# A transformer layer in float32 on one core: when DMA-made weight sums of the first Strassen group are loaded

## Chip, core and metric

The kernel runs on one core of a Trainium2 chip. The metric is the device time of one execution in microseconds (us). Before the change it is 1293.23 us, the median of three runs (1292.48 to 1294.61). Engines are named as the profile names them: PE (TensorE, matmuls), DVE (VectorE), ACT (ScalarE), POOL (GpSimd), SP (SyncE, which here only issues DMAs). A DMA that adds to its destination is issued by POOL.

## What is computed

One layer on x of 512 tokens by 1024 features, all in float32:

```python
x = x + 0.5 * swiglu(rmsnorm(x, ffn1_norm), ffn1_w1, ffn1_w3, ffn1_w2)   # first feed-forward
h = rmsnorm(x, mix_norm)
x = x + hybrid_mixer(h, w_in, ...)          # dilated attention, grouped-query attention, gates
x = x + 0.5 * swiglu(rmsnorm(x, ffn2_norm), ffn2_w1, ffn2_w3, ffn2_w2)   # second feed-forward
return rmsnorm(x, final_norm)

def swiglu(x, w1, w3, w2):                  # w1, w3: 1024 x 2816, w2: 2816 x 1024
    return (silu(x @ w1) * (x @ w3)) @ w2
```

## The kernel before

**Products.** Each product of float32 numbers is made of three matmuls of a shorter format: an operand is split into a high part H (a copy on ACT, `wh` for weights, L211) and a low part L (a subtraction on DVE, `wl`, L212), and `mm3` (L226 to L228) adds H·H, L·H and H·L in a PSUM bank. A weight tile is thus loaded (512 KB), cast on ACT, split on DVE, and then used by 24 matmuls on PE. The split tiles have a ring of three buffers (`wh`), so a tile's cast waits until PE has finished with the tile three before it; in feed-forward stages every fourth tile of the order uses a buffer of its own (`whx`).

**A feed-forward stage** (`ffn_run`) has a plain part and groups. In the plain part of the first feed-forward (stage "a") eight weight tiles, the first four feature blocks of w1 and w3, are multiplied with the 512 tokens, 24 matmuls of 128x512 each; the first two go pairwise. The four banks of `mm` rotate. A finished bank is emptied on DVE by `done1` (L445: times R, the norm's factor per token) or `done3` (L449), with a silu on ACT between. R comes late: the squares are summed, POOL takes the power (L380, `r`), PE transposes it (L395, `rb`), ACT copies it to R (L397). Until then the four banks are full.

**The groups** make blocks of w1 and w3 by a Strassen scheme, two at a time (f and f+1) in seven steps of 24 matmuls of 128x256: A11, S1, S2, A12, S3, S4, A22. GROUPS gives the groups' ends: in stage "a" the first group has f = 4 and 6, in stage "b" (the second feed-forward) f = 2, 4 and 6; the second starts at f = 8 in both. The weights of the steps are:

- A11 and A12: a plain load by SP (L190) into one of three `wa` tiles; A22 into a `wr` tile;
- S1 and S3: sums of two quarters, made by DMA in one of four `wt` tiles. SP loads the first quarter (L192); when that has landed POOL issues an accumulating DMA of the second (L193);
- S2 = S1 + A11 and S4 = S2 + A12: sums on DVE (L210, `ws`).

**The order of the loads.** `Layer.order` lists all weight tiles as PE uses them, numbered n. In stage "a" n = 0 to 7 are the plain tiles; the first group has n = 8 (A11 of f=4), 9 (S1), 10 (S2), 11 (A12), 12 (A11 of f=6), 13 (S3 of f=4), 14 (S1 of f=6), up to 21. `todo` (L117) is the sequence in which the loads are written into the program: by n, but a `wt` tile is sorted as if it were EARLY steps sooner. `loads` takes from its head as long as the ring has a tile. PE's order is the program's own; on the other engines a scheduler sets the order when the program is built, from the sequence in which it was written and its own estimate of when inputs are there. Each engine and each queue then runs strictly in that order.

```python
EARLY = {"a": 6, "b": 6, "q": 4}
GROUPS = {"a": (4, 8, 16, 22), "b": (2, 8, 16, 22)}
...
self.todo = sorted((n for n, t in enumerate(self.kind) if t != "ws"),
                   key=lambda n: n - (EARLY[self.order[n][0][2]] if self.kind[n] == "wt" else 0))
```

Of the kernel before, what the change touches and what calls it, by code (L numbers as in the profile page):

```python
# [16 lines left out]
DRAM = bass.MemoryType.DRAM  # L17

BUFS = {"wr": 3, "wa": 3, "ws": 2, "wt": 4, "wh": 3, "whx": 1}
EARLY = {"a": 6, "b": 6, "q": 4}  # L20
GROUPS = {"a": (4, 8, 16, 22), "b": (2, 8, 16, 22)}
PAIRS = ((0, 0), (1, 0), (0, 1), (0, 2), (1, 1), (1, 2), (2, 0), (3, 0), (2, 1), (2, 2), (3, 1), (3, 2))
NSQ = 10
# [46 lines left out]
class Layer:  # L70
    def __init__(self, ctx, tc, a):
        self.tc, self.nc, self.a = tc, tc.nc, a
        ctx.enter_context(tc.manual_schedule(engines={mybir.EngineType.PE}))
        pool = lambda n, **k: ctx.enter_context(tc.tile_pool(name=n, **k))
        self.dram = pool("dram", bufs=1, space=DRAM)
        self.cst = pool("cst", bufs=1)
        self.wb = pool("wb", bufs=1)
        self.tmp = pool("tmp", bufs=4)
        self.psm = pool("psm", bufs=4, space=PSUM)
        self.psa = pool("psa", bufs=4, space=PSUM)  # L80
        nc = self.nc
        c = self.cst
        self.x = [c.tile([128, T], F32, name=f"x{d}") for d in range(NK)]
        self.par = c.tile([128, 48], F32, name="par")
        nc.scalar.dma_start(self.par, a["par"])
        self.ident = c.tile([128, 128], F32, name="ident")
        self.ones = c.tile([128, 1], F32, name="ones")
        nc.vector.memset(self.ones, 1.0)
        self.mhalf = c.tile([128, 4], F32, name="mhalf")
        nc.vector.memset(self.mhalf, -0.5)  # L90
        nc.scalar.activation(self.ones, self.ones, AF.Copy)
        self.r = c.tile([128, 8], F32, name="r")
        self.R = c.tile([128, T], F32, name="R")
        nc.gpsimd.memset(self.R, 0.0)
        self.acc = c.tile([128, T], F32, name="acc")
        self.open_h()
        self.gate_d = self.dram.tile([16, 128, T], F32, name="gate_d")
        self.qk_d = self.dram.tile([2 * NSQ, 128, T], F32, name="qk_d")
        self.items = ([("v", 0), ("v", 1), ("sw", 0), ("v", 2)] + [("g", j) for j in range(2)]
                      + [("qk", f) for f in range(NSQ, 12)] + [("g", j) for j in range(2, 9)]  # L100
                      + [("b", g) for g in range(3)] + [("g", j) for j in range(9, 16)])
        span = {"v": ("wav", 4), "qk": ("waq", 2), "g": ("wg", 1), "b": ("wb", 4)}
        self.order = self.ffn_order("a")
        for kind, n in self.items:
            if kind == "sw":
                self.order += [("swq", at) for at in self.slots(range(0, NSQ, 2))]
                continue
            name, m = span[kind]
            self.order += [(name, m * n + i) for i in range(m)]
        self.order += [("wab", i) for i in range(12)] + [("wo", i) for i in range(8)]  # L110
        self.order += self.ffn_order("b")
        self.raws, self.tiles, self.used, self.wx, self.TQ = {}, [], 0, None, None
        self.cap = len(self.order)
        self.rings = {k: [] for k in BUFS}
        self.index = {it[:2]: n for n, it in enumerate(self.order)}
        self.kind = [self.home(it) for it in self.order]
        self.todo = sorted((n for n, t in enumerate(self.kind) if t != "ws"), key=lambda n: n - (EARLY[self.order[n][0][2]] if self.kind[n] == "wt" else 0))  # L117

    @staticmethod
    def slots(fs):  # L120
# [1098 lines left out]
```

## Time and profile before

| | |
|---|---|
| median of three runs | 1293.23 us |
| the profiled execution | 1292.9 us |
| its span | 1291.1 us |
| PE busy | 1270.1 us (98%) |
| DVE, ACT, POOL busy | 889.5, 587.0, 118.5 us |
| mean granted clock of PE | 0.993 of full speed |
| moved by DMA | 181.91 MB, mean 141 GB/s |

The profile is of one execution. A row gives a start and a duration in us from the span's start; in brackets stands how long the engine was idle before, and what ended that. PE's rows overlap, since matmuls are pipelined: from start to start counts. The granted clock is the share of TensorE's full 2.4 GHz; 0.50 is its lower level, 1.2 GHz.

### The profile page before, as it was taken

The numbers are of one execution on the slowest core, as the hardware profiler recorded it, in microseconds if no ns is written. First come the engines' busy times: TensorE is split into PE (matmuls) and PEld (weight loads), VectorE is DVE, ScalarE is ACT, GpSimd is POOL, SyncE is SP. The second block draws the span as 40 slices with busy tenths as digits, with TensorE's granted clock in tenths as the row PEclk, the third lists the DMA queues.
The fourth block names the chain that finished last, engine by engine and source line by source line (L and its number), as shares of the span: only waits on it lengthen the run. The fifth ranks groups of instructions, "written<-read, shape, count | busy, mean of one in ns | idle before, by whom it ended". The sixth has DMA issues, their size and how long they took to land.

```text
span 1291.1 us, 19957 instructions
## 1 busy us (share of the span) xinstructions
PE 1270.1 (98%) x8002; PEld 1123.6 (87%) x8002; DVE 889.5 (69%) x1339; ACT 587.0 (45%) x867; POOL 118.5 (9%) x124
## 2 busy tenths in 40 slices
PE   8799999999999999999999999999999999999997
PEld 6697899899889999877888878888889989988996
DVE  7576588557783787576647898655677756874775
ACT  7352255235463443545424455543465415542553
POOL 1011011000120111200001100000301000100001
PEclk9899999999999999999999999999999999999998
DMA  9665776341474854733232221245826626743221
GB/s 290 185 153 158 216 185 181 125 115 34 130 216 128 235 168 137 253 107 92 85 125 67 81 82 41 92 161 158 259 82 180 189 89 173 196 154 98 67 82 66
DMA packets 85549, 181.91 MB, mean 141 GB/s; under 512 B 12480, under 2 KB 19024, under 8 KB 85456
## 3 DMA queue, kind: packets, MB, share of 16 engines
q1 hardware_dynamic: 67904, 140.74, 32.8%
q0 software_dynamic: 16832, 39.34, 14.9%
q8 instruction: 63, 1.03, 0.3%
q10 hardware_dynamic: 720, 0.55, 0.1%
q14 instruction: 30, 0.25, 0.1%
HBM read 168.98 MB, written 15.29 MB: 143 GB/s over the span
## 4 chain that ended last, share of the span: by engine, by line
PE 92%; DVE 3%; DMA 2%; ACT 1%; issue 1%; SPq 0%; POOL 0%; POOLq 0%; DVEq 0%
PE mm L226 24%; PE mm L227 23%; PE mm L228 23%; PE Y L226 3%; PE Y L227 3%; PE Y L228 3%; PE X L226 2%; PE X L228 2%; PE X L227 2%; PE S L779 1%; PE mm L830 1%; PE Tb L969 1%; PE T L848 1%; DMA wa<-in_w13a 1%; DVE wl L212 1%
## 5 line engine op out<-in xcount | busy, mean ns | idle before, releaser
L211 ACT CAST wh<-wr 128x1024 fp32r<-128x1024 f32 x142 | 148.9, 1049 | 223.9 <-PE mm L227 147.7
L212 DVE TENSOR_TENSOR wl<-wr,wh 128x1024 fp32r<-128x1024 f32 x142 | 173.6, 1223 | 56.8 <-ACT wh L211 56.4
L226 PE MATMUL mm<-hH,wh 128*128 128x256 f32 (+1 forms) x600 | 201.6, 336 | 8.0 <-DVE t L445 7.6
L228 PE MATMUL mm<-hH,wl 128*128 128x256 f32 (+1 forms) x600 | 197.3, 329 | 0.9 <-DVE wl L212 0.9
L227 PE MATMUL mm<-hL,wh 128*128 128x256 f32 (+1 forms) x600 | 197.2, 329 | 0.3 <-DVE hL L363 0.3
L226 PE MATMUL mm<-gg,wh 128*128 128x512 f32 (+1 forms) x376 | 143.1, 381 | 0.0
L228 PE MATMUL mm<-gg,wl 128*128 128x512 f32 (+1 forms) x376 | 142.6, 379 | 0.0
L227 PE MATMUL mm<-gg,wh 128*128 128x512 f32 (+1 forms) x376 | 142.5, 379 | 0.0
L226 PEld LDWEIGHTS mm<-hH,wh 128*128 128x128 f32 x600 | 113.4, 189 | 23.1 <-DVE t L445 8.0
L228 PEld LDWEIGHTS mm<-hH,wl 128*128 128x128 f32 x600 | 113.4, 189 | 12.6 <-DVE wl L212 1.3
L227 PEld LDWEIGHTS mm<-hL,wh 128*128 128x128 f32 x600 | 113.4, 189 | 10.5 <-DVE hL L363 0.9
L211 ACT CAST wh<-wa 128x1024 fp32r<-128x1024 f32 x48 | 50.4, 1049 | 108.7 <-PE mm L227 49.7
L494 DVE TENSOR_TENSOR u<-mm,R 128x512 f32<-128x512 f32 (+1 forms) x52 | 33.8, 649 | 85.0 <-PE mm L228 84.7
L212 DVE TENSOR_TENSOR wl<-wt,wh 128x1024 fp32r<-128x1024 f32 x48 | 58.7, 1223 | 38.1 <-ACT wh L211 37.6
L228 PE MATMUL mm<-TH,wl 128*128 128x256 f32 x304 | 84.7, 279 | 0.0
L226 PE MATMUL mm<-TH,wh 128*128 128x256 f32 x304 | 84.6, 278 | 0.0
L227 PE MATMUL mm<-TL,wh 128*128 128x256 f32 x304 | 84.6, 278 | 0.0
L226 PEld LDWEIGHTS mm<-gg,wh 128*128 128x128 f32 x376 | 70.8, 188 | 15.2 <-PE mm L228 0.9
L228 PEld LDWEIGHTS mm<-gg,wl 128*128 128x128 f32 x376 | 70.8, 188 | 14.1
L227 PEld LDWEIGHTS mm<-gg,wh 128*128 128x128 f32 x376 | 70.9, 188 | 13.8
L211 ACT CAST wh<-ws 128x1024 fp32r<-128x1024 f32 x48 | 50.4, 1051 | 71.0 <-PE mm L227 52.3
L212 DVE TENSOR_TENSOR wl<-wa,wh 128x1024 fp32r<-128x1024 f32 x48 | 58.6, 1222 | 31.6 <-ACT wh L211 31.4
(233 smaller groups left out, 3172.0 us busy)
## 6 DMA issues: line engine op xcount, KB each, us to landing
wr<-in_w2a SPq DMA_DIRECT2D x22, 512.0 KB, 3.3
wr<-in_w2b SPq DMA_DIRECT2D x22, 512.0 KB, 3.3
wt<-in_w13b SPq DMA_DIRECT2D x20, 512.0 KB, 3.8
wt<-in_w13b POOLq DMA_DIRECT2D x20, 512.0 KB, 5.7
wa<-in_w13b SPq DMA_DIRECT2D x20, 512.0 KB, 4.0
wt<-in_w13a SPq DMA_DIRECT2D x18, 512.0 KB, 3.5
wt<-in_w13a POOLq DMA_DIRECT2D x18, 512.0 KB, 6.3
wa<-in_w13a SPq DMA_DIRECT2D x18, 512.0 KB, 3.3
```

The source lines that it names most:

```text
L211: self.nc.scalar.copy(H, raw)
L212: self.nc.vector.tensor_sub(L, raw, f32(H))
L226: mm(out, lH, rH, start=start, stop=False, skip_group_check=more)
L227: mm(out, lH, rL, start=False, stop=False, skip_group_check=more)
L228: mm(out, lL, rH, start=False, stop=stop, skip_group_check=more)
L494: nc.vector.tensor_mul(u, ps, R)
L779: nc.tensor.matmul(*args, start=True, stop=True)
L830: nc.tensor.matmul(oc, v, p, start=st, stop=sp)
L848: nc.tensor.transpose(ps[:, 128 * b:128 * b + 128], P[h][:, c0 + 128 * b:c0 + 128 * b + 128], self.ident)
L969: nc.tensor.transpose(pt[:, 128 * j:128 * j + 128], P[h, j][:, 128 * k:128 * k + 128], self.ident)
```

## The change

The lead of a `wt` load becomes a function of its group: six steps from the second group of a feed-forward stage on (f of 8 or more), four in the first group. The projection stage "q" keeps four. The four `wt` tiles stay. Two pairs in stage "a" and three in stage "b" are concerned, with two `wt` tiles each.

```diff
-EARLY = {"a": 6, "b": 6, "q": 4}
+EARLY, EARLIER = 4, 6
...
-        self.todo = sorted((n for n, t in enumerate(self.kind) if t != "ws"), key=lambda n: n - (EARLY[self.order[n][0][2]] if self.kind[n] == "wt" else 0))
+        self.todo = sorted((n for n, t in enumerate(self.kind) if t != "ws"), key=self.turn_of)
+
+    def turn_of(self, n):
+        if self.kind[n] != "wt":
+            return n
+        s, f = self.order[n][0][2], self.order[n][1][0]
+        return n - (EARLIER if s != "q" and f >= GROUPS[s][1] else EARLY)
```

All lines behind L117 have numbers six higher in the changed kernel (L445 is L451 there). PE's rows are the same in both, one by one. The other engines' rows move at two places only: around the end of the plain part of the first feed-forward, and, on SP alone, ahead of the second one.

SP, the loads ahead of the first Strassen group, from the first `wt` load on. `wr` are plain tiles; `wa_299` is A11 of f=4 (`wa_296` in the change), `wa_304` A12 of f=4, `wa_306` A11 of f=6; `wt_200` is S1 and `wt_296` S3 of f=4 (`wt_208` and `wt_298` in the change), `wt_301` and `wt_308` those of f=6. Before:

```order
L192 DMA wt_200<-in_w13a 128x2x512
L180 DMA wr_198<-in_w13a 128x1024
L180 DMA wr_203<-in_w13a 128x1024
L180 DMA wr_209<-in_w13a 128x1024
L192 DMA wt_296<-in_w13a 128x2x512
L180 DMA wr_215<-in_w13a 128x1024
L180 DMA wr_294<-in_w13a 128x1024
L190 DMA wa_299<-in_w13a 128x2x512
L192 DMA wt_301<-in_w13a 128x2x512
L190 DMA wa_304<-in_w13a 128x2x512
L190 DMA wa_306<-in_w13a 128x2x512
L192 DMA wt_308<-in_w13a 128x2x512
```

With the change:

```order
L198 DMA wt_208<-in_w13a 128x2x512
L186 DMA wr_198<-in_w13a 128x1024
L186 DMA wr_200<-in_w13a 128x1024
L186 DMA wr_206<-in_w13a 128x1024
L196 DMA wa_296<-in_w13a 128x2x512
L186 DMA wr_215<-in_w13a 128x1024
L186 DMA wr_294<-in_w13a 128x1024
L198 DMA wt_298<-in_w13a 128x2x512
L198 DMA wt_301<-in_w13a 128x2x512
L196 DMA wa_304<-in_w13a 128x2x512
L196 DMA wa_306<-in_w13a 128x2x512
L198 DMA wt_308<-in_w13a 128x2x512
```

The load of S3 went from ahead of two plain tiles to behind them, and A11 took its place. The A12 tile `wa_304` has the same ten loads ahead of it from `wr_196` on. POOL's half of the moved sum went with it, from ahead of the power L380 to behind it; and behind these rows the next `wa` load, A12 of f=6, went behind two `wr` loads.

ACT, from the cast of the sixth plain tile on, around the copy of R. `wh_554` is the cast of the A12 tile, in the extra buffer; `t1_379` and `t1_386` are what `done1` makes of the first and second blocks, `gg_383` their products' casts, `wh_404` the seventh plain tile. Before:

```order
L211 CAST wh_350<-wr_209 128x1024
L322 CAST TH_185<-T1_315 128x1024 x2
L211 CAST wh_554<-wa_304 128x1024
L397 COPY R_91<-rb_373 128x512
L446 ACT_TABLE_LOAD
L446 ACTIVATE t1_379<-t1_379 128x512
L446 ACTIVATE t1_386<-t1_386 128x512
L211 CAST wh_404<-wr_215 128x1024
L429 CAST gg_383<-t1_379 128x512
L429 CAST gg_383<-t1_386 128x512
```

With the change:

```order
L217 CAST wh_350<-wr_206 128x1024
L328 CAST TH_185<-T1_315 128x1024
L403 COPY R_91<-rb_373 128x512
L328 CAST TH_185<-T1_315 128x1024
L452 ACT_TABLE_LOAD
L452 ACTIVATE t1_379<-t1_379 128x512
L452 ACTIVATE t1_386<-t1_386 128x512
L217 CAST wh_404<-wr_215 128x1024
L217 CAST wh_554<-wa_304 128x1024
L435 CAST gg_383<-t1_379 128x512
L435 CAST gg_383<-t1_386 128x512
```

The cast of the A12 tile went from ahead of the copy of R to behind both silus and the seventh plain tile's cast, and one of the two TH casts went behind the copy.

DVE, from the last transform of the activations (T1) on. `TL` are low parts of the transformed activations, `ws_544` and `ws_685` the sums S2 and S4 of f=4. Before:

```order
L331 SCALAR_TENSOR_TENSOR T1_315<-T1_315 128x1024
L323 TENSOR_TENSOR TL_186<-T1_315,TH_185 128x1024
L210 TENSOR_TENSOR ws_544<-wt_200,wa_299 128x1024
L323 TENSOR_TENSOR TL_186<-T1_315,TH_185 128x1024
L210 TENSOR_TENSOR ws_685<-ws_544,wa_304 128x1024
L212 TENSOR_TENSOR wl_555<-wa_304,wh_554 128x1024
L445 TENSOR_TENSOR t1_379<-mm_217,R_91 128x512
L445 TENSOR_TENSOR t1_386<-mm_289,R_91 128x512
```

With the change:

```order
L337 SCALAR_TENSOR_TENSOR T1_315<-T1_315 128x1024
L451 TENSOR_TENSOR t1_379<-mm_217,R_91 128x512
L451 TENSOR_TENSOR t1_386<-mm_289,R_91 128x512
L329 TENSOR_TENSOR TL_186<-T1_315,TH_185 128x1024
L455 SCALAR_TENSOR_TENSOR t1_379<-mm_218,t1_379 128x512
L455 SCALAR_TENSOR_TENSOR t1_386<-mm_349,t1_386 128x512
L218 TENSOR_TENSOR wl_405<-wr_215,wh_404 128x1024
```

Both multiplications with R (L451) went ahead of the two TL splits, the two sums and the split of the A12 tile. The second TL split, the sums and that split follow further down, among the next plain tiles' splits.

## Rows read from the trace of the kernel before

**Rows 1.** From the page: the span, the busy time of the engines (share, instructions), and the first of the three kinds of matmuls on hH, of plain and Strassen steps together (busy us, mean ns, idle time before, its releaser).
```profile
span 1291.1 us, 19957 instructions
PE 1270.1 (98%) x8002; PEld 1123.6 (87%) x8002; DVE 889.5 (69%) x1339; ACT 587.0 (45%) x867; POOL 118.5 (9%) x124
...
L226 PE MATMUL mm<-hH,wh 128*128 128x256 f32 (+1 forms) x600 | 201.6, 336 | 8.0 <-DVE t L445 7.6
```

**Rows 2.** The longest of PE's waits in the whole span (us in total, times, longest).
```profile
PE mm L226 <- DVE t L445: 7.6, 1, 7.6
```

**Rows 3.** The chain of waits that ended last in the stretch from 22 to 64 us (start, us, what), around its longest piece.
```profile
26.10 9.80 DMA wa<-in_w13a
36.00 1.23 DVE ws L210
37.23 1.14 DVE wl L212
38.36 0.61 DVE t L445
39.01 0.80 PE mm L226
```

**Rows 4.** Four stretches: length, busy time of PE, PEld, DVE, ACT and POOL with instructions, then PE's granted clock, the mean DMA share, and GB/s.
```profile
20.00:30.00 10.00, 10.00 (x51) 8.24 (x50) 9.21 (x10) 6.62 (x8) 2.81 (x2) 1.00 0.99 314
31.25:39.01 7.76, 0.17 (x1) 0.00 (x0) 5.17 (x6) 2.83 (x4) 1.24 (x1) 0.74 1.09 299
39.01:45.15 6.14, 6.14 (x14) 4.79 (x15) 4.27 (x6) 3.19 (x5) 1.20 (x1) 0.50 1.04 263
45.15:63.93 18.78, 18.78 (x83) 15.40 (x82) 7.78 (x11) 6.15 (x10) 0.00 (x0) 1.00 0.40 124
```

**Rows 5.** PE's timeline in the first feed-forward: a short wait, R's transposes, the last matmul ahead of the long wait, the first one at full speed behind it, and the first matmuls of the Strassen steps A11 and S1.
```profile
19.15 0.51 PE L228 MATMUL mm<-hH,wl 128*128 128x512 f32 x1 [0.88 <-DVE wl L212]
...
28.69 0.65 PE L395 MATMUL rb<-ident,r 128*128 128x128 f32 x4
...
31.02 0.40 PE L228 MATMUL mm<-hH,wl 128*128 128x512 f32 x1
...
45.15 0.39 PE L228 MATMUL mm<-hH,wl 128*128 128x512 f32 x1
...
63.93 0.28 PE L226 MATMUL mm<-hH,wh 128*128 128x256 f32 x1
...
66.76 0.28 PE L226 MATMUL Y<-TH,wh 128*128 128x256 f32 x1
```

**Rows 6.** ACT's timeline around the copy of R.
```profile
30.03 1.05 ACT L322 CAST TH<-T 128x1024 fp32r<-128x1024 f32 x1 [2.30 <-DVE T L331]
35.93 1.04 ACT L211 CAST wh<-wa 128x1024 fp32r<-128x1024 f32 x1 [4.84 <-DMA wa<-in_w13a]
36.88 0.58 ACT L397 COPY R<-rb 128x512 f32<-128x512 f32 x1
37.48 1.28 ACT L446 ACT_TABLE_LOAD   x1
38.99 1.23 ACT L446 ACTIVATE t<-t 128x512 f32<-128x512 f32 x2 [0.23 <-DVE t L445]
...
41.06 1.13 ACT L429 CAST gg<-t 128x512 fp32r<-128x512 f32 x2
```

**Rows 7.** DVE's timeline around L445, and the sum S4 of f=6.
```profile
28.79 1.21 DVE L331 SCALAR_TENSOR_TENSOR T<-T 128x1024 f32<-128x1024 f32 x1
...
36.00 1.23 DVE L210 TENSOR_TENSOR ws<-ws,wa 128x1024 f32<-128x1024 f32 x1 [2.59 <-DMA wa<-in_w13a]
37.14 1.22 DVE L212 TENSOR_TENSOR wl<-wa,wh 128x1024 fp32r<-128x1024 f32 x1
38.28 1.28 DVE L445 TENSOR_TENSOR t<-mm,R 128x512 f32<-128x512 f32 x2
...
77.61 1.22 DVE L210 TENSOR_TENSOR ws<-ws,wa 128x1024 f32<-128x1024 f32 x1
```

**Rows 8.** SP's issues ahead of the first group: the second `wt` load, A11, and the A12 of f=4 with the load after it.
```profile
19.50 0.48 SPq L192 DMA_DIRECT2D wt<-in_w13a  x1
...
24.11 1.42 SPq L190 DMA_DIRECT2D wa<-in_w13a  x1
...
26.10 1.18 SPq L190 DMA_DIRECT2D wa<-in_w13a  x2
```

**Rows 9.** POOL's timeline: the issue of the fourth accumulating DMA of the group.
```profile
41.11 1.20 POOL L193 DMA_DIRECT2D wt<-in_w13a  x1 [7.30 <-DMA wt<-in_w13a]
```

**Rows 10.** The loads of `wa` tiles in the first 130 us, from issue to landing.
```profile
DMA to landing us min/median/max: 3.3/6.1/9.8
```

**Rows 11.** The loads of `wt` tiles in the first 130 us, both halves, from issue to landing.
```profile
DMA to landing us min/median/max: 3.4/5.9/10.5
```

**Rows 12.** The stretch around the start of the second feed-forward, columns as in rows 4.
```profile
880.00:960.00 80.00, 80.00 (x354) 65.15 (x353) 50.15 (x56) 37.15 (x48) 13.71 (x10) 1.00 0.57 175
```

**Rows 13.** SP's issues ahead of the second feed-forward: the first two `wt` loads, and the first `wa` load.
```profile
894.15 0.94 SPq L192 DMA_DIRECT2D wt<-in_w13b  x2
...
900.50 1.12 SPq L190 DMA_DIRECT2D wa<-in_w13b  x1
```

**Rows 14.** The wait of the norm's power on POOL between 900 and 960 us (us in total, times, longest).
```profile
POOL r L380 <- DVE ms L379: 13.8, 1, 13.8
```

## Prediction

> **What bounds the kernel now.** I read the first page for the shares, then the list of PE's waits, the chain of waits around the longest of them, and then the four engines' timelines and the queues over that stretch.
>
> PE is busy for 1270.1 of the 1291.1 us [rows 1], so the only time to be had lies in PE's 21 us without work and in matmuls that ran slowly. One wait is most of it: 7.6 us, once, in front of a matmul of the first feed-forward, released by the DVE line L445 [rows 1, 2]. The chain shows what L445 itself waited for [rows 3]: the load of a wa tile took 9.80 us, from 26.10 to 35.9; then came the sum L210, the split L212 and L445, and at 39.01 PE went on.
>
> That wa tile is A12 of f=4, needed by PE only in the Strassen group, tens of us later. What PE needed at 31 us was a free bank: the plain stage's fifth weight tile reuses the first pair's bank, which L445 empties. L445 needs R, and R is copied by ACT (L397). On ACT the cast of the wa tile stood ahead of that copy, and idled 4.84 us for the load, until 35.93 [rows 6]; on DVE the sum ws<-ws,wa stood ahead of L445 and started at 36.00 for the same load [rows 7]. R's transposes on PE had been there since 28.69 + 0.65 = 29.3 [rows 5]. So two in-order engines stood in front of a load that nobody needed yet.
>
> The wait has a second price. In the 6.14 us after it the granted clock was 0.50, the lower level of 1.2 GHz; then 1.00 [rows 4]. PE had been without a matmul for the 7.6 us before. The 14 matmuls of that stretch took 6.14 us. At full clock 82 starts took 18.78 us, 0.229 each [rows 4, 5], so 14 would take 3.20.
>
> **The change part by part.** *On ACT* the copy of R moves ahead of the wa cast, which now stands behind both silus and the cast of the next plain tile. *On DVE* both L445 move ahead of two TL splits, the two sums and the split of the wa tile. Nothing is added or removed; PE's order is the same row for row. The new times, each from its row:
>
> - ACT: it is free from the first TH cast before 29.3, so R is copied from about 29.4 to 30.0 (0.58, [rows 6]).
> - DVE: the transform L331 ends at 28.79 + 1.21 = 30.0 [rows 7]. The first L445 (half of the 1.28 us of two, 0.64) ends at about 30.7.
> - PE: its last matmul starts at 31.02 [rows 5], so the next is due at 31.25. The bank is free 0.5 us before. No wait, and no fall of the clock behind it.
> - The next tile, due 24 × 0.229 = 5.5 us later, at 36.7, needs the bank of the pair's second product. ACT makes the other TH cast (30.03 + 1.05), the table load (1.28) and the silu (0.62) by 33.0 [rows 6]; the DVE multiplication, like L445 about 0.65, ends at 33.7. Margin 3 us.
> - The tile after that, due at 42.2, needs its cast and split: the cast like the one at 35.93 takes 1.04, behind the two silus it ends at 34.7, and the split (1.22, [rows 7]) at 35.9. Margin 6 us.
> - The last plain tile, due at 47.7, has its cast behind the moved wa cast and two gg casts (1.13, [rows 6]). If the wa load lands as before, at 35.9, that cast ends at about 39.2 and the split at about 41. Margin over 6 us.
>
> What is moved behind L445 takes DVE 2 × 1.21 + 2 × 1.22 + 1.22, about 6 us. It falls between 31 and 50 us; before, DVE worked 7.78 of the 18.78 us up to 63.93 [rows 4], which is the cover. If that cover were short the first to be late would be the splits of the Strassen tiles, due from 53 us on.
>
> *The first Strassen step* then starts at 31.25 + 96 × 0.229 = 53.2 in place of 63.93 [rows 5]. The gain is the wait, 39.01 − 31.25 = 7.76, plus the slow matmuls, 6.14 − 3.20 = 2.94: **10.7 us**.
>
> *The queues.* On SP the A11 load takes the second wt load's place at 19.50 and that load moves to about 24, past two wr loads [rows 8]. The A12 load that made the wait has ten loads of 512 KB ahead of it in either order, so I take no gain from an earlier landing. On POOL the accumulating half of the moved sum goes behind the power L380. It used to be issued ahead of it; that can bring R's transposes forward by some tenths at most, since they also stand behind PE's matmuls; I count 0 and keep 0.3 for the range. A later wa load (A12 of f=6) waits for the buffer that the split at 37.14 sets free, so it was issued at 38.4 [rows 7]; that split now follows the last plain tile's (41) and one sum, 1.23 + 1.22 later, so it is issued near 44. With the longest landing of such a load, 9.8 [rows 10], it is there by 54, and its first reader, the sum at 77.61 [rows 7], moves to 66.9: covered by 13 us.
>
> *The sums themselves.* Four steps of lead instead of six: a step is 66.76 − 63.93 = 2.83 us [rows 5], so the lead shrinks by 5.7 us. The trace has no late sum in this group to price that. Its cover: the last of the four is issued on POOL at 41.11 [rows 9], and with the longest landing, 10.5 [rows 11], is in place by 53, while the first moved one is wanted in the sixth step, 53.2 + 5 × 2.83 = 67.4. The nearest rows leave over 10 us, so 0.
>
> A rule of the Trainium skill speaks against this part: its page "DMA: Bandwidth & Descriptors", section "Rules for kernel authors", says to issue a DMA early and wait for it late, so that its fixed cost overlaps. By it a load issued 4.6 us later costs up to that, and the sum would be 6.1 instead of 10.7; rows 8 to 11 show cover and not cost.
>
> *The second feed-forward* has the same edit for three pairs. On SP the first wa load moves ahead of an output-projection load and the second wt load behind it, where they stood at 900.50 and 894.15 [rows 13]. ACT and DVE keep their order there. PE is busy 80.00 of the 80 us from 880 to 960 at full clock [rows 12]: no gain to be had. A loss needs a wait that is not there now; the sums' POOL queue also carries the squares for the norm, and behind them the power idled 13.8 us [rows 14], so a sum late by less than that costs nothing. I take 0; both ends go into the range with some tenths.
>
> **Sum.** The profiled execution took 1292.9 us, 1.8 around its span of 1291.1. 1292.9 − 10.7 = 1282.2. The median of the three runs is 0.33 above the profiled one, so I say 1282.4.
>
> **Rivals.**
> - *A short wait stays.* The margin at 31.25 is 0.5 us. If R or L445 comes 1 to 3 us late, PE waits that long. A wait of 0.88 us at 19.15 [rows 5] left the clock at 1.00 [rows 4], so this alone gives 1283.4 to 1285.4, or up to 1288 if the clock falls all the same. For it: DVE has no idle time before 30.0. Against: both moved engines were early before. Chance 0.07.
> - *The sums come late* (the page's rule, as a mechanism here): the moved load reaches PE late in the sixth Strassen step by up to the 4.6 us that it is moved, plus 2.9 of low clock: 1287 to 1290. Against it the 10 us of cover. Chance 0.03.
> - *It gives nothing.* PE reaches the Strassen group 10.7 us sooner, while the queues move 263 to 299 GB/s at full DMA share until 45 us [rows 4]; loads whose time does not move with PE could take the gain back, or the scheduler's order does not act as read: about 1293. Against: every load needed before 70 us is issued by 45. Chance 0.06.
> - *Slower.* The wa cast now stands ahead of the cast of the last plain tile. That cast must start by 47.7 minus 1.13, 1.04, 1.22 and the wa cast's own 1.04, so the A12 load must land by 43. Beyond, PE waits a us for each us, plus 2.9 of low clock. The gain is used up if it lands at 51, and the kernel is over 0.2% slower from about 54: some 28 us after its issue, where the longest such load took 9.8. At 55 us: about 1297. Chance 0.04.
>
> **How the numbers follow.** The forecast as worked out has 0.80. A measurement of this kernel tells 0.2%, 2.6 us, from no change. Faster by more holds the forecast and the first two rivals: 0.80 + 0.07 + 0.03 = 0.90; same 0.06; slower 0.04. The range goes down by the run spread and the tenths of POOL to 1280.5, and up over most of the short-wait case and the start of the late-sum case to 1287.0, leaving out little over 0.10.
>
> **What the profile of the changed kernel would show.** Right: PE's list of waits without the 7.6 us; the copy of R at about 29.5 and the first L451 at 30 (the lines are six higher); granted clock 1.00 from 31 to 63; the first 128x256 matmul at about 53.2; ACT idling for the wa load, if at all, behind the silus and without PE waiting. Wrong: a PE wait between 31 and 53, a gap in the Strassen steps released by a wt or wa load, or the second feed-forward with a wait that it did not have. A time above 1290 would mean that the gain was given back behind 64 us, and the chain of waits would name the load.

## The result, and the profile after

The changed kernel takes 1282.69 us in the median of four runs (1281.67 to 1282.82); the kernel before, also of four, 1292.99 (1292.48 to 1294.61). The ratio is 0.9916, with a 95% interval of 0.9899 to 0.9934. The prediction was 1282.4, with a range of 1280.5 to 1287.0 and a chance of 0.90 for faster.

The first page of the kernel after, the span, the engines' busy time and the first group of matmuls (columns as in [rows 1]):

```profile
span 1281.0 us, 19956 instructions
PE 1266.8 (99%) x8002; PEld 1122.1 (88%) x8002; DVE 887.8 (69%) x1339; ACT 586.5 (46%) x867; POOL 118.9 (9%) x124
...
L232 PE MATMUL mm<-hH,wh 128*128 128x256 f32 (+1 forms) x600 | 200.5, 334 | 0.4 <-ACT hH L368 0.3
```

Against [rows 1] the span is 10.1 us shorter, the instructions of each engine are the same in number, and the idle time ahead of this group fell from 8.0 to 0.4 us. PE's busy time fell too, by 3.3 us, though it has the same 8002 instructions: most of that is the matmuls that ran slowly [rows 4].

PE's list of waits over the whole span, the four longest:

```profile
PE mm L836 <- DVE PT L856: 1.6, 1, 1.6
PE warm L1101 <- POOL R L94: 1.3, 1, 1.3
PE rb L401 <- POOL r L386: 1.0, 1, 1.0
PE mm L234 <- DVE wl L218: 1.0, 1, 1.0
```

The 7.6 us behind L445 [rows 2] has no successor: L451, as that line is called now, isn't in the list. Three stretches of the first feed-forward, and one around the start of the second (columns as in [rows 4]):

```profile
31.00:39.00 8.00, 8.00 (x36) 6.57 (x35) 6.86 (x10) 6.96 (x9) 3.65 (x3) 1.00 1.08 323
39.00:45.00 6.00, 6.00 (x28) 4.91 (x27) 6.00 (x7) 1.99 (x3) 0.00 (x0) 1.00 1.11 259
45.00:53.50 8.50, 8.50 (x39) 6.98 (x38) 4.75 (x8) 3.35 (x8) 0.00 (x0) 1.00 0.72 244
...
880.00:960.00 80.00, 80.00 (x374) 66.17 (x374) 51.84 (x61) 40.71 (x56) 15.16 (x11) 1.00 0.57 170
```

PE is busy throughout, and the granted clock is 1.00 where it had been 0.74 and 0.50 [rows 4]. The last line answers to [rows 12]: around the start of the second feed-forward PE is busy for all of the 80 us, as before. PE's timeline at the places of [rows 5]:

```profile
19.46 0.50 PE L234 MATMUL mm<-hH,wl 128*128 128x512 f32 x1 [0.99 <-DVE wl L218]
...
28.95 0.60 PE L401 MATMUL rb<-ident,r 128*128 128x128 f32 x4
...
31.24 0.39 PE L234 MATMUL mm<-hH,wl 128*128 128x512 f32 x1
31.46 0.39 PE L232 MATMUL mm<-hH,wh 128*128 128x512 f32 x1
...
53.44 0.28 PE L232 MATMUL mm<-hH,wh 128*128 128x256 f32 x1
```

Where PE had stopped at 31.25 it goes on without a gap, and the first Strassen matmul stands at 53.44 in place of 63.93. ACT and DVE around it, to be held against [rows 6] and [rows 7]:

```profile
29.64 0.59 ACT L403 COPY R<-rb 128x512 f32<-128x512 f32 x1 [1.62 <-PE rb L401]
30.54 1.05 ACT L328 CAST TH<-T 128x1024 fp32r<-128x1024 f32 x1 [0.31 <-DVE T L337]
31.61 1.28 ACT L452 ACT_TABLE_LOAD   x1
32.90 1.15 ACT L452 ACTIVATE t<-t 128x512 f32<-128x512 f32 x2
33.96 1.03 ACT L217 CAST wh<-wr 128x1024 fp32r<-128x1024 f32 x1
34.90 1.05 ACT L217 CAST wh<-wa 128x1024 fp32r<-128x1024 f32 x1
```
```profile
29.29 1.22 DVE L337 SCALAR_TENSOR_TENSOR T<-T 128x1024 f32<-128x1024 f32 x1
30.43 1.28 DVE L451 TENSOR_TENSOR t<-mm,R 128x512 f32<-128x512 f32 x2
31.63 1.21 DVE L329 TENSOR_TENSOR TL<-T,TH 128x1024 fp32r<-128x1024 f32 x1
33.57 1.29 DVE L455 SCALAR_TENSOR_TENSOR t<-mm,t 128x512 f32<-128x512 f32 x2 [0.73 <-ACT t L452]
...
40.58 1.22 DVE L216 TENSOR_TENSOR ws<-wt,wa 128x1024 f32<-128x1024 f32 x1
...
42.85 1.22 DVE L216 TENSOR_TENSOR ws<-ws,wa 128x1024 f32<-128x1024 f32 x1
```

The cast of A12 runs at 34.90 without waiting: by the time that ACT comes to it the load is there. The sums that had stood ahead of L445 run at 40.58 and 42.85.

### The profile page after: what moved, and what is told of

Read it like the earlier page. It is cut to its first block, busy times and chain, and to the rows that moved or that the text cites. A ratio compares the mean times of both kernels' runs of the same rounds, so it can differ in the third digit from the quotient of the medians.

```text
span 1281.0 us, 19956 instructions
## 1 busy us (share of the span) xinstructions
PE 1266.8 (99%) x8002; PEld 1122.1 (88%) x8002; DVE 887.8 (69%) x1339; ACT 586.5 (46%) x867; POOL 118.9 (9%) x124
## 4 chain that ended last, share of the span: by engine, by line
PE 93%; DVE 3%; issue 1%; DMA 1%; ACT 1%; POOL 0%; SPq 0%; POOLq 0%; DVEq 0%
PE mm L232 24%; PE mm L234 24%; PE mm L233 24%; PE Y L232 3%; PE Y L234 3%; PE Y L233 3%; PE X L232 2%; PE X L234 2%; PE X L233 2%; PE S L785 1%; PE mm L836 1%; PE Tb L975 1%; PE T L854 1%; PE Sb L233 0%; PE Sb L234 0%
## 5 line engine op out<-in xcount | busy, mean ns | idle before, releaser
L233 PEld LDWEIGHTS mm<-hL,wh 128*128 128x128 f32 x600 | 112.8, 188 | 10.1 <-DVE hL L369 0.8
```

The source lines that it names most:

```text
L233: mm(out, lH, rL, start=False, stop=False, skip_group_check=more)
```

## Experiments

The theory, T1: the time was lost in the order of two in-order engines, ACT's cast of A12 ahead of the copy of R and DVE's sum with A12 ahead of L445, so that a load that nobody needed yet held up PE. Its rival, T2: the loads themselves matter (when they are issued and land, or which tiles there are). A held-back instruction in the diffs below (`behind(on, x)`) keeps its data and its loads; it only takes its place in its engine's row behind x. `muls[1]` is the second L445 (L459 in the first three runs; the number changes with the lines put in), `rcopy` the copy of R, `cast6` the cast of the seventh plain tile; the tiles n = 10, 11 and 15 are S2, A12 and S4 of f=4. "Before" is what the kernel before took beside each. The last column counts PE's wait for that multiplication alone; what PE waited elsewhere is in the text.

| run | edit against | median us (lowest to highest) | before | ratio, 95% interval | longest wait for L445 |
|---|---|---|---|---|---|
| e1_pin_both | before | 1283.84 (1282.62 to 1284.39) | 1293.38 | 0.9927 [0.9915, 0.9940] | none |
| e2_pin_act | before | 1292.32 (1291.03 to 1293.71) | 1293.38 | 0.9990 [0.9981, 0.9998] | 5.29 |
| e3_pin_dve | before | 1292.67 (1290.65 to 1293.99) | 1293.38 | 0.9993 [0.9984, 1.0002] | 3.96 |
| e6_lead0 | after | 1293.92 (1292.36 to 1296.12) | 1293.38 | 1.0007 [0.9998, 1.0016] | 8.56 |
| e4_a_only | after | 1282.82 (1282.29 to 1282.98) | 1293.51 | 0.9913 [0.9899, 0.9927] | none |
| e5_b_only | after | 1293.42 (1291.94 to 1294.85) | 1293.51 | 1.0000 [0.9991, 1.0008] | 7.99 |
| e8_pin_three | before | 1282.12 (1281.96 to 1282.46) | 1293.51 | 0.9908 [0.9895, 0.9922] | none |
| e9_lead0_pinned | after | 1282.56 (1281.98 to 1282.92) | 1293.51 | 0.9911 [0.9897, 0.9924] | none |
| e6_lead2 | after | 1282.50 (1281.90 to 1282.98) | 1293.82 | 0.9913 [0.9899, 0.9926] | none |

### The order alone, with before's loads

e1_pin_both leaves the loads that SP issues ahead of the first Strassen group in the order of the kernel before, and holds back what stood ahead of the copy of R and of L445:

```diff
-            self.nc.vector.tensor_add(raw, a, b)
-        self.nc.scalar.copy(H, raw)
-        self.nc.vector.tensor_sub(L, raw, f32(H))
+            with self.behind(DVE_PIN and n in (10, 15), self.muls[1]):
+                self.nc.vector.tensor_add(raw, a, b)
+        with self.behind(ACT_PIN and n == 11, self.cast6):
+            cast = self.nc.scalar.copy(H, raw)
+        if n == 6:
+            self.cast6 = cast
+        with self.behind(DVE_PIN and n == 11, self.muls[1:2] and self.muls[1]):
+            self.nc.vector.tensor_sub(L, raw, f32(H))
...
-            nc.scalar.copy(H, src)
-            nc.vector.tensor_sub(L, src, f32(H))
+            with self.behind(ACT_PIN and g == G_FFN1 and c == 2, self.rcopy):
+                nc.scalar.copy(H, src)
+            with self.behind(DVE_PIN and g == G_FFN1 and c > 1, self.muls[1:2] and self.muls[1]):
+                nc.vector.tensor_sub(L, src, f32(H))
```

> The loads stay as before the change (lead of six steps everywhere, the same issues in the same order ahead of the first group); ACT and DVE alone are put in the changed kernel's order around the copy of R: the A12 cast behind the copy and the silus, the TL splits, the two sums and the A12 split behind both multiplications with R. Theory 1 (the gain is the order of ACT and DVE in front of a load that nobody needs yet): PE goes on at about 31.3 us without a wait, the clock does not fall, about 1282.7 us. Theory 2 (the gain is on the queues: the moved loads let others land sooner): nothing gained, about 1293 us.

It took 1283.84 us: nine tenths of the gain with the loads ahead of the wait in their old order. T2's 1293 is out. The copy of R and both multiplications run before the cast of A12, which has hardly moved (35.93 before):

```profile
30.34 0.59 ACT L411 COPY R<-rb 128x512 f32<-128x512 f32 x1 [2.83 <-PE rb L409]
...
35.70 1.05 ACT L220 CAST wh<-wa 128x1024 fp32r<-128x1024 f32 x1
```
```profile
30.96 1.29 DVE L459 TENSOR_TENSOR t<-mm,R 128x512 f32<-128x512 f32 x2 [1.18 <-ACT R L411]
```

One load further on moved by itself: A12 of f=6 waits for the buffer that the held-back split frees, and was issued at 44.29 in place of 38.39, as with the change. It moved in e3_pin_dve too (to 52.30), where next to nothing was gained.

The missing 1.1 us were not in T1's number; POOL and PE show where part of them sits:

```profile
26.73 1.21 POOL L195 DMA_DIRECT2D wt<-in_w13a  x1 [9.02 <-DMA wt<-in_w13a]
27.58 1.96 POOL L394 TENSOR_TENSOR r<-ms,mhalf 128x4 f32<-128x4 f32 x1
```
```profile
29.60 0.65 PE L409 MATMUL rb<-ident,r 128*128 128x128 f32 x4 [0.99 <-POOL r L394]
...
54.14 0.28 PE L238 MATMUL mm<-hH,wh 128*128 128x256 f32 x1
```

The accumulating DMA, still ahead of the norm's power on POOL, waited for its first half until 26.73; the power followed, and R's transposes on PE waited 0.99 for it.

### Each engine alone

e2_pin_act and e3_pin_dve are the same kernel with one of the two switches on:

```diff
-ACT_PIN, DVE_PIN = True, True
+ACT_PIN, DVE_PIN = True, False    # e2_pin_act; False, True in e3_pin_dve
```

> As the run with both engines reordered, but ACT alone; DVE keeps the sum ws<-ws,wa ahead of the multiplication with R. Theory 1: the sum still waits for the A12 load until about 36, 1.2 us of sum and 0.65 us of multiplication follow, PE goes on at about 37.8 instead of 39.0, with the low clock behind: about 1291.7 us. If ACT alone had been what held PE: about 1283 us. Theory 2: about 1293 us.

> As the run with both engines reordered, but DVE alone; ACT keeps the A12 cast ahead of the copy of R. Theory 1: R is still copied only from 36.9 to 37.5, PE goes on at about 38.2, low clock behind: about 1292.1 us. If DVE alone had been what held PE: about 1283 us. Theory 2: about 1293 us.

Each gives next to nothing alone. In e2 R is there at 30.44 + 0.59, and DVE's rows say what L459 still stood behind:

```profile
30.97 1.21 DVE L218 TENSOR_TENSOR ws<-wt,wa 128x1024 f32<-128x1024 f32 x1
35.84 1.23 DVE L218 TENSOR_TENSOR ws<-ws,wa 128x1024 f32<-128x1024 f32 x1 [3.66 <-DMA wa<-in_w13a]
36.99 1.28 DVE L459 TENSOR_TENSOR t<-mm,R 128x512 f32<-128x512 f32 x2
```
```profile
37.72 0.80 PE L238 MATMUL mm<-hH,wh 128*128 128x512 f32 x1 [5.29 <-DVE t L459]
```

PE went on at 37.72, where 37.8 was expected. In e3 DVE was free and idle for R, which ACT could not give it:

```profile
37.34 1.04 ACT L220 CAST wh<-wa 128x1024 fp32r<-128x1024 f32 x1 [5.80 <-DMA wa<-in_w13a]
38.29 0.58 ACT L411 COPY R<-rb 128x512 f32<-128x512 f32 x1
```
```profile
38.90 1.29 DVE L459 TENSOR_TENSOR t<-mm,R 128x512 f32<-128x512 f32 x2 [8.44 <-ACT R L411]
```

Here PE went on at 39.65, 1.4 later than expected, since in this run the load landed at 37.3 and not at 35.9:

```profile
31.42 1.12 PE L409 MATMUL rb<-ident,r 128*128 128x128 f32 x4 [2.13 <-POOL r L394]
...
34.82 0.39 PE L238 MATMUL mm<-hH,wh 128*128 128x512 f32 x1
...
39.65 0.79 PE L238 MATMUL mm<-hH,wh 128*128 128x512 f32 x1 [3.96 <-DVE t L459]
```

The 3.96 us look short beside the 7.60 before, and are no gain: PE came late to them. It had waited 2.13 at R's transposes, for POOL's power, and then ran at a granted clock of 0.50 for some 3 us. In e2 it had waited 1.00 at the same place. So the two engines are two gates in front of one load, in parallel: the wait ends with the later of the two, and opening one gives at most their difference. The medians are 1.06 us below the kernel before in e2, and 0.71 in e3, which its interval does not tell from none.

### POOL's place

e8_pin_three is e1_pin_both with the accumulating DMA of that one sum issued behind the power:

```diff
-            nc.gpsimd.dma_start(dst, part("A22" if step == "S1" else "A11"), accum_op=ALU.add)
+            add = lambda: nc.gpsimd.dma_start(dst, part("A22" if step == "S1" else "A11"), accum_op=ALU.add)
+            if POOL_PIN and n == 13 and name == "sw" + "a":
+                self.held_add = add
+            else:
+                add()
...
-        nc.gpsimd.tensor_tensor(dst, ms, self.mhalf[:, :n], op=ALU.pow)
+        power = nc.gpsimd.tensor_tensor(dst, ms, self.mhalf[:, :n], op=ALU.pow)
+        if self.held_add:
+            add, self.held_add = self.held_add, None
+            with self.tc.issue_after(power.ins):
+                add()
```

> The loads on SP as before the change, ACT and DVE in the changed kernel's order as in the run with both reordered, and on POOL also the accumulating DMA of the second sum behind the power, as the change has it. That run had PE waiting 1.0 us for the power at R's transposes and reached the first Strassen matmul at 54.14 where the changed kernel did at 53.44. If POOL's order is what is left between them: no such wait, 53.4, and 1282.7 us. If it is the landing of the loads: 54.1 again, and 1283.8 us.

```profile
25.87 1.95 POOL L398 TENSOR_TENSOR r<-ms,mhalf 128x4 f32<-128x4 f32 x1 [7.96 <-DVE ms L397]
27.78 1.24 POOL L195 DMA_DIRECT2D wt<-in_w13a  x1
```

The power starts 1.71 us sooner, the transposes stand at 28.98 without a wait, and the first 128x256 matmul at 53.47 in place of e1's 54.14. The time is 1282.12, as fast as the changed kernel. Its rows on ACT, DVE and POOL are the changed kernel's, one by one, while SP's loads ahead of the first group, and in the second feed-forward, stand in the order of the kernel before. Of the 1.7 us between the medians of e1 and e8, beside which the kernel before took 1293.38 and 1293.51, 0.67 is seen at this place, and 0.3 more in the attention's wait for PT (1.2 in e1, 0.9 here), which differs between runs anyhow; the rest isn't placed.

### The two feed-forwards apart

e4_a_only makes the change in the first feed-forward only, e5_b_only in the second only:

```diff
-        return n - (EARLIER if s != "q" and f >= GROUPS[s][1] else EARLY)
+        return n - (EARLIER if s == "b" or s == "a" and f >= GROUPS[s][1] else EARLY)    # e4_a_only
+        return n - (EARLIER if s == "a" or s == "b" and f >= GROUPS[s][1] else EARLY)    # e5_b_only
```

> The change in the first feed-forward alone; the second keeps six steps in its first group too. ACT, DVE and POOL then have the changed kernel's rows one by one. Theory 1: all of the gain, 1282.7 us. If the second feed-forward's loads had a part of it: above 1283.5 us.

> The change in the second feed-forward alone. Theory 1: PE has no wait there to lose, and the 7.6 us wait of the first stays: no difference, 1293.2 us. If the second feed-forward had a part: below 1292 us.

All of it is in the first (1282.82), nothing in the second (ratio 1.0000). In e5 the old wait stands as before, 7.99 us behind L451 in this run.

### How late may a sum be loaded

e6_lead2 and e6_lead0 shorten the first groups' lead from four steps to two and to none:

```diff
-        return n - (EARLIER if s != "q" and f >= GROUPS[s][1] else EARLY)
+        return n - (EARLY if s == "q" else EARLIER if f >= GROUPS[s][1] else 0)    # e6_lead0; 2 in e6_lead2
```

> The first group's sums get no lead at all (sorted by their own step), six steps from the second group on. The rows show the A12 cast ahead of the copy of R on ACT again, and sum and A12 split ahead of the multiplications on DVE, while A12 has two loads fewer ahead of it. Theory 1: the load lands some 3.3 us sooner (two loads of 512 KB at about 315 GB/s), near 32.6; cast, split and sum follow; PE goes on near 36.8 with the low clock behind: about 1290.8 us. Theory 2 (fewer early loads are better): 1282.7 us or less. If the sums came late: PE waits in the Strassen steps of the first group, released by a wt tile.

The expectation missed: 1293.92 in place of 1290.8, and PE went on at 40.07 and not at 36.8. The A12 load came early enough (its cast ran at 30.25, the copy of R at 32.14), but DVE's rows showed another load to wait for:

```profile
30.08 1.21 DVE L329 TENSOR_TENSOR TL<-T,TH 128x1024 fp32r<-128x1024 f32 x1
34.78 1.23 DVE L216 TENSOR_TENSOR ws<-wt,wa 128x1024 f32<-128x1024 f32 x1 [3.49 <-DMA wt<-in_w13a]
...
38.19 1.22 DVE L216 TENSOR_TENSOR ws<-ws,wa 128x1024 f32<-128x1024 f32 x1
39.33 1.28 DVE L451 TENSOR_TENSOR t<-mm,R 128x512 f32<-128x512 f32 x2
```

The sum S2, made from the now late `wt` tile, stands ahead of L451 and waits for that tile until 34.78; PE waits 8.56 us. One can read this two ways: a late sum costs time, or only its place in DVE's row does. e9_lead0_pinned tells them apart: the loads of e6_lead0, with the copy of R and the multiplications held ahead on ACT and DVE by the edit of e1.

> No lead at all for the first groups' sums, with ACT and DVE in the changed kernel's order. In the run without lead and without that order, DVE's sum S2 waited 3.5 us for a sum made by DMA, ahead of the multiplications with R, and PE waited 8.6 us. Theory 1: the sums behind the multiplications harm nobody; PE has no wait, about 1282.7 us. If the sums now come too late for the Strassen steps themselves: waits there released by a wt tile, 1285 us or more.

```profile
36.17 2.55 POOL L201 DMA_DIRECT2D wt<-in_w13a  x2 [8.37 <-DMA wt<-in_w13a]
40.23 1.20 POOL L201 DMA_DIRECT2D wt<-in_w13a  x1 [1.51 <-DMA wt<-in_w13a]
```

The first accumulating DMA of the group is issued at 24.60 and the fourth at 40.23, against 16.11 and 36.76 with the change, and PE has no wait between 20 and 64 us; the time is 1282.56. So it was the place alone.

> The change with a lead of two steps instead of four in a feed-forward stage's first group (six from the second group on, four tiles). ACT's row then has the copy into R of the next tile, then the cast of A12, then the table load and the two silus; before's had the cast ahead of the copy, the change's has it behind the silus. T1 (what costs is only what stands ahead of the copy and of L451): the copy starts near 29.6 us as with the change, the cast may wait for its load until 31 to 36 us, and the silus end by about 34 to 39 us; if A12 has landed by 33 us PE does not wait, the first 128x256 matmul stands near 53.4 us and the time is about 1282.7 us; if it lands at 36 us the second silu is late, PE waits some 2 us for L455, and the time is 1285 to 1288 us. T2 (sums need their lead): the second sum of the Strassen step is late, PE waits in the Strassen steps behind 53 us, and the time is above 1287 us.

This one came between: the order that the scheduler made puts A12's cast ahead of the silus, and the load is waited for, but behind the copy:

```profile
29.70 0.59 ACT L403 COPY R<-rb 128x512 f32<-128x512 f32 x1 [1.62 <-PE rb L401]
30.86 1.05 ACT L217 CAST wh<-wa 128x1024 fp32r<-128x1024 f32 x1 [0.57 <-DMA wa<-in_w13a]
31.81 1.05 ACT L217 CAST wh<-wr 128x1024 fp32r<-128x1024 f32 x1
32.88 1.28 ACT L452 ACT_TABLE_LOAD   x1
34.18 1.15 ACT L452 ACTIVATE t<-t 128x512 f32<-128x512 f32 x2
```

A load waited for 0.57 us cost nothing, L455 ran at 34.84 before it was due, and the time is T1's: 1282.50. With leads of zero, two and four steps, and of six with all three orders held, the kernel takes 1282.1 to 1282.8 wherever the copy of R and L451 stand ahead of what waits, and 1292 to 1294 wherever they don't; e1, with POOL's order left as it was, stands between at 1283.84.

## Why the prediction was right, point by point

- **The cause.** Right, and shown: order without loads gives the gain (e1, e8), other leads without that order give none (e6_lead0).
- **The wait, 7.76 us, and the slow clock, 2.94.** The first Strassen matmul was put at 53.2 and stood at 53.44: 10.5 of the 10.7 us are seen there. The other 0.2 arose ahead of the change's place: the short wait of [rows 5] ended at 19.46 and not at 19.15, and from there on PE was some 0.2 to 0.3 later, at R's transposes too (28.95 and not 28.69).
- **The margins.** L451's first half was to end at 30.7, half a microsecond before it was due; it ended at about 31.1 (30.43 and half of 1.28), due at 31.46, so the margin was 0.4. The DVE transform ahead of it ended at 30.5 and not 30.0: 0.3 of that was there at the transform before it (25.67 and not 25.38), and 0.2 came from a split that stood behind an ACT cast, which had waited 1.16 for a `wr` load. L455's first half ended near 34.2 (33.7 said), and the last plain tile's split at 40.7 (41). The rival "a short wait stays" was near: 0.4 us more and PE would have waited. Its price would not have been its lower end alone: in e3 a wait of 2.13 at R's transposes was enough for the granted clock to fall to 0.50, and cost 1.57 more.
- **A12's landing.** Taken as 35.9; it was there by 34.90. It was right to take no gain from it: the cast isn't on the path.
- **POOL.** This is the term that was mis-sized. Moving the accumulating DMA behind the power was counted 0, with 0.3 for the range. That was true of the profiled execution of before, where that DMA was issued at 25.82 and the transposes had no wait. With the same order on POOL it was issued at 25.75 in e5, again without a wait; at 26.19 in e2 and 26.73 in e1, and the transposes waited 1.00 and 0.99; at 28.83 in e3, and they waited 2.13. What the gain is without POOL's move the nearest run says, e1 at 1283.84: inside the range, but 1.4 above the forecast. The sum came out because the change has the move and the trace that it was read from happened to have no such wait; that forecast and median agree to 0.3 us is in part luck.
- **The sums come late.** The prediction set the rows' cover of over 10 us against the rule of the Trainium skill ("DMA: Bandwidth & Descriptors", "Rules for kernel authors") to issue a DMA early and wait late. The rows were right here, by more than was claimed: with no lead at all e9 loses nothing. The rule's second half is the one that the kernel before broke, with the wait and not with the issue: A12 was waited for early, ahead of urgent work.
- **The second feed-forward.** 0, as said: PE 80.00 of 80 us, and e5 at a ratio of 1.0000.
- **It gives nothing.** Nearly all of the gain lasted to the end: 10.49 us at the first Strassen matmul, 10.1 in the span. Behind that matmul the distance between PE's rows in the two kernels changes by more than 0.2 us at one place only, the attention's wait for PT. That wait (L856) is 1.6 us where it was 1.1. It does not follow the change: it was 0.8 in e4, whose first feed-forward is the changed kernel's, 1.5 in e2, and from 0.8 to 1.6 over all runs here. What sets it was not tried.
- **Slower.** Its mechanism, A12 landing after 43, has no example: its latest landing in any run here is 37.3.

## What to carry to other kernels

When a busy engine waits, go back through the rows of the in-order engines that release it, and ask of every instruction that stands ahead of the release and itself waits for a load: who needs its result, and when? If that is late, move it behind; if several engines each have such an instruction, all must be moved, or next to nothing is gained. A load's lead is not only a matter of when its data come: the scheduler also makes another order of the engines from it. Here leads of six and of none gave orders in which PE waited, two and four gave orders in which it did not, and with the order held six and none did no harm. So a change of the lead should be read in the engines' orders before it is read in the queue.

## What was not expected of the hardware

- **The price of the slow clock does not follow the length of the wait.** From the first matmul behind the wait to the first 128x256 one there are 96 starts, 21.98 us at full clock (31.46 to 53.44 in the kernel after). It took 24.92 behind the wait of 7.60 in the kernel before, so 2.94 lost; 2.82 behind 8.56 (e6_lead0), 2.59 behind 5.29 (e2), 2.56 behind 3.96 (e3), but 1.73 behind 7.99 (e5). At R's transposes a wait of 0.99 (e1) left the clock at 1.00, and one of 2.13 (e3) did not: from the transposes to the seventh matmul behind them took 3.40 us (31.42 to 34.82) in place of 1.83 (28.95 to 30.78 in the kernel after), so 1.57 lost. e3's 2.56 came on top of that.
- **One load's landing moves by several microseconds** at a full DMA share. A12 of f=4, issued at 26.10 in the kernel before, landed 9.8 us later, at 35.9; with the same loads ahead of it on SP it took 10.3 us in e5 (issued at 25.87), 11.8 in e3 (25.50), and 7.8 in e8 (26.05). In e6_lead2, with two loads fewer ahead of it, it was issued at 24.31 and took 6.5. Which neighbours in the queue make the difference was not tried.
